# Matmuls over 64 rows grouped by twos of upper and lower halves, and the last steps before the experts' second table reordered

## The chip, the cores and the metric

One core of one Trainium2 chip runs the kernel. The metric is the device time of the whole program in microseconds (us), lower is better. The core has a matrix engine (PE, with its weight loads, PEld, shown apart), a vector engine (DVE), a scalar engine (ACT), GpSimd (POOL), and SyncE (SP), which issues DMAs. SBUF is the working memory of 128 partitions; PSUM, in eight banks, takes what PE writes.

## The reference

A decoder layer over 256 tokens of width 1024, all in float32:

```
h = rmsnorm(x);  proj = h @ w_in        # retention q,k,v,gate | attention q,k,v | two merge gates
A = groupnorm(retention(rq, rk, rv)) * silu(rg) @ ret_w_branch    # 8 heads, keys of 64, values of 128
B = softmax(mq mk^T + bias, causal) mv @ moba_w_branch            # 8 heads of 64
x = x + (sigmoid(ga) * A + sigmoid(gb) * B) @ w_out
h2 = rmsnorm(x)                         # then experts: 8 heads pick 16 of 16384 each
x = x + sum over picked e of gate_e * gelu(h2 . u[e]) * v[e]
```

Retention works in two chunks of 128 tokens: scores inside a chunk times a decay, and for the second chunk a product with the state that the first one left (`kv`).

## The kernel before

The program is one long list of instructions, in the order in which the Python code makes them; each engine takes its own in that order.

**Mixer** (to about 262 us). The projections are split into pieces of 256 rows of weights. For each piece `i` the loop loads, cuts the float32 weights into two parts (`cut`: ACT line 146, DVE line 147), does 12 matmuls (`products`, L229 to L231 or L238 to L240) and then calls `pump()`. `pump` takes one step of each of up to three tasks: Python generators that stop at each `yield`. Such a step is called a visit here. `attention()` and `retention()` are tasks. Their small matmuls go into PSUM tiles `side`, a ring of four banks; DVE or ACT then takes the bank's content away.

Heads of width 64 lie by twos in 128 partitions: head half `c = 0` in partitions 0 to 63, `c = 1` in 64 to 127 (`b = slice(c * 64, (c + 1) * 64)`). So attention's scores (L360), retention's scores (L423) and the product with the state (L440) are matmuls over 64 rows. All others near them are over 128 rows. A float32 matmul of the program stands as two instructions in the trace. Before the change a visit deals with one half at a time; in retention, L438 (128 rows) and L440 (64 rows) take turns into the same piece of a bank.

**Experts**. For 128 chunks `c` of the table u (loop at L1209): chunk's load, transposes (L711), products (L1224). Beside it the rows that some tokens picked are fetched one by one (`fetch`, a POOL DMA, L990) and used on DVE: `gather_step()` makes one fetch and one use, `gather(n)` adds `n` to a credit and makes a step for each whole one. For rows of v the use is a sum (L1075, into `accx` and then `vacc`), which comes six fetches later. In the last chunks the first pieces of the second phase are prepared: `cut_v` splits a chunk of v (ACT L146, DVE L147), `cut_w` a pair of columns of the gate matrix W (ACT L1197, DVE L1198). The place where the loop over u ends and the one over v (L1261) begins is called the seam. In the loop over v each chunk has 16 matmuls (L1257, L1258), or plain ones (L1255) for ten pairs of chunks, and a `gather(GATHER_V)`.

Of the kernel before, what the change touches and what calls it, by code (L numbers as in the profile page):

```python
# [19 lines left out]
OP = mybir.AluOpType  # L20
AX = mybir.AxisListType

P = 128
S = 256
# [3 lines left out]
H = 8  # L28
NK = 128
# [7 lines left out]
NW = NG + NXP * NXV  # L37
ND = S - NW
RING = 6
GATHER_V = 0.6  # L40
GATHER = 1.04
GATHER_G = 1.36
RAWS = 6
# [31 lines left out]
def layer_kernel(ctx, tc, x, mix_norm_g, w_in, ret_w_branch, moba_q_gain, moba_k_gain, moba_w_branch,  # L75
# [3 lines left out]
    V, A, G, T = nc.vector, nc.scalar, nc.gpsimd, nc.tensor  # L79
# [16 lines left out]
    def side():  # L96
        return psum.tile([P, 512], F32, name="side", bufs=4)
# [83 lines left out]
    def t4(shape, name, dt=F32):  # L181
        return wk.tile(shape, dt, name=name, tag="t4", bufs=3)
# [75 lines left out]
    bias = ap.tile([P, H, S], F32, name="bias", tag="b8d")  # L258
# [90 lines left out]
    def attention():  # L349
        ssum = wk.tile([P, NT, H], F32, name="ssum")  # L350
        for t in range(NT):
            w = (t + 1) * P
            pr = wk.tile([P, H, S], F32, name="pr")
            nh = 512 // w
            for i0 in range(0, H, nh):
                p = side()
                for j in range(nh):
                    c, hp = divmod(i0 + j, 4)
                    b = slice(c * 64, (c + 1) * 64)
                    T.matmul(p[:, j * w:(j + 1) * w], mqk[0][b, hp, t * P:(t + 1) * P], mqk[1][b, hp, :w],  # L360
                             start=True, stop=True)
                V.tensor_tensor(pr[:, i0:i0 + nh, :w], p.rearrange("p (j k) -> p j k", j=nh),
                                bias[:, i0:i0 + nh, S - w:], op=OP.add)
                yield
            sm = wk.tile([P, H], F32, name="smx")
            V.tensor_reduce(sm, pr[:, :, :w], axis=AX.X, op=OP.max, negate=True)
            for h in range(H):
                A.activation(pr[:, h, :w], pr[:, h, :w], AF.Exp, bias=sm[:, h:h + 1], accum_out=ssum[:, t, h:h + 1])
                if h % 4 == 3:
                    yield  # L370
            rs = wk.tile([P, H], F32, name="rs")
            V.reciprocal(rs, ssum[:, t, :])
            yield
            po = side()
            for kt in range(t + 1):
                prT = t4([P, H, P], "prT")
                for q in range(2):
                    p = side()
                    for j in range(4):
                        T.transpose(p[:, j * P:(j + 1) * P], pr[:, 4 * q + j, kt * P:(kt + 1) * P], ident)  # L380
                    A.activation(prT[:, 4 * q:4 * q + 4, :], p.rearrange("p (j i) -> p j i", j=4), AF.Copy)
                yield
                for i in range(H):
                    h = 2 * (i % 4) + i // 4
                    T.matmul(po[:, h * 64:(h + 1) * 64], prT[:, i, :], mv[:, kt, h * 64:(h + 1) * 64],
                             start=(kt == 0 and i == 0), stop=(kt == t), skip_group_check=True)
            at = t2([P, 512], "at")
            for c in range(2):
                V.tensor_tensor(at.rearrange("p (i c d) -> p c i d", c=2, d=64)[:, c],
                                po.rearrange("p (i c d) -> p c i d", c=2, d=64)[:, c],  # L390
                                rs[:, 4 * c:4 * c + 4, None].to_broadcast([P, 4, 64]), op=OP.mult)
            yield
            p = side()
            for c in range(4):
                T.transpose(p[:, c * P:(c + 1) * P], at[:, c * P:(c + 1) * P], ident)
            split_to(ah[0][:, :, t * P:(t + 1) * P], al[0][:, :, t * P:(t + 1) * P],
                     p.rearrange("p (c q) -> p c q", c=4))
            yield
# [7 lines left out]
    def retention():  # L406
        for q in range(2):
            p = side()
            for j in range(2):
                hp = 2 * q + j  # L410
                T.matmul(p[:, j * S:(j + 1) * S], kdec[:, hp * P:(hp + 1) * P], rv[0][:, hp * S:(hp + 1) * S],
                         start=True, stop=True)
            A.activation(kv[:, 2 * q:2 * q + 2, :], p.rearrange("p (j e) -> p j e", j=2), AF.Copy)
            yield
        for t in range(NT):
            s = slice(t * P, (t + 1) * P)

            st = t4([P, H, P], "st")
            for c in range(2):
                b = slice(c * 64, (c + 1) * 64)  # L420
                p = side()
                for j in range(4):
                    T.matmul(p[:, j * P:(j + 1) * P], rqk[1][b, j, s], rqk[0][b, j, s], start=True, stop=True)  # L423
                V.tensor_tensor(st[:, 4 * c:4 * c + 4, :], p.rearrange("p (j i) -> p j i", j=4),
                                decay[:, 4 * c:4 * c + 4, :], op=OP.mult)
                yield
            st6 = wk.tile([P, H, 6], F32, name="st6")
            mvv = wk.tile([P, H, 2], F32, name="mvv")
            va = wk.tile([P, H], F32, name="va")
            nm = wk.tile([P, H], F32, name="nm")  # L430
            os_ = []
            for c in range(2):
                b = slice(c * 64, (c + 1) * 64)
                p = side()
                for j in range(4):
                    h = 2 * j + c
                    d = p[:, j * P:(j + 1) * P]
                    T.matmul(d, st[:, 4 * c + j, :], rv[t][:, h * P:(h + 1) * P], start=True, stop=(t == 0))  # L438
                    if t:
                        T.matmul(d, rqdT[b, j, :], kv[b, j, c * P:(c + 1) * P], start=False, stop=True)  # L440
                for j in range(4):
                    V.bn_stats(st6[:, 4 * c + j, :], p[:, j * P:(j + 1) * P])
                os_.append(p)
                yield
            for i in range(H):
                V.bn_aggr(mvv[:, i, :], st6[:, i, :])
            V.tensor_scalar(va, mvv[:, :, 1], EPS, None, op0=OP.add)  # L447
            r = rsqrt_(wk, va, [P, H], "gn")
            yield
            V.scalar_tensor_tensor(nm, mvv[:, :, 0], -1.0, r, op0=OP.mult, op1=OP.mult)  # L450
            for c in range(2):
                for j in range(4):
                    h, i = 2 * j + c, 4 * c + j
                    A.activation(ret[:, t, h * P:(h + 1) * P], os_[c][:, j * P:(j + 1) * P], AF.Identity,
                                 bias=nm[:, i:i + 1], scale=r[:, i:i + 1])
                yield
# [301 lines left out]
    for t in range(NT):  # L758
        for q in range(2):
# [4 lines left out]
            p = side()  # L764
# [422 lines left out]
    def cut_v(c):  # L1187
        if c < NK:
            hi, lo = hi_tile(), lo_tile()
            split_to(hi, lo, v_raw.pop(c))  # L1190
            v_cut[c] = (hi, lo)

    def cut_w(c):

        if c < NK:
            w = cw[:, c // 2 % 2]
            A.activation(w[:, :, :ND], W[:, c:c + 2, :], AF.Copy)  # L1197
            V.tensor_tensor(w[:, :, ND:], W[:, c:c + 2, :], w[:, :, :ND].bitcast(F32), op=OP.subtract)  # L1198
            w_cut[c] = w
# [9 lines left out]
    for c in range(NK):  # L1209
        load_to(len(pieces) + c + TAHEAD)  # L1210
        rows_x(c)
        gates_finish()
        transpose_u(c + TAHEAD)
        if c and c % 2 == 0:
            product_evac(c - 2, pa)
        if c == SCRATCH:
            while any(g in chain for g in topk_all):
                chain_step(1.0)
        if c % 2 == 0:
            pa = acc(0)  # L1220
        uT = u_T.pop(c)
        for k in range(KC):
            n = c % 2 * NA
            T.matmul(pa[:, n:n + NA], uT[:, k * P:(k + 1) * P], hTf[:, k], start=(c % 2 == 0 and k == 0),  # L1224
                     stop=(k == KC - 1), skip_group_check=True)
        pump()
        if c < NK - 3:
            gather(gs["pace"])
        chain_step(BUDGET)

        if c == NK - 4:
            while chain:
                chain_step(9.0)
                gates_finish()
            cw = cp.tile([P, 2, D], F32R, name="cw", tag="b8")[:, :, :4 * ND].rearrange("p s (c t) -> p s c t", c=2)
        if c >= NK - 3:
            load_to(len(pieces) + c + 3)
        if c == NK - 3:
            cut_v(0)
        elif c == NK - 2:  # L1240
            cut_w(0)
        elif c == NK - 1:
            cut_v(1)
    product_evac(NK - 2, pa)

# [136 lines left out]
```

## Time and profile before

| | us |
|---|---|
| median of 3 runs | 975.61 (974.99 to 977.25) |
| the profiled execution | 976.44 |
| its span in the trace | 974.7 |
| PE busy in the span | 965.4 |

The rows below come from the one profiled execution. Its time is its span and 1.74 us around it. [...]

### The profile page before, as it was taken

Reading aid. Unit: us, or ns where it says so; the run is one execution under the profiler, and the core shown is the slowest. Engines: PE = TensorE matmul, PEld = TensorE weight load, DVE = VectorE, ACT = ScalarE, POOL = GpSimd, SP = SyncE. Lnnn points to the kernel's source line nnn. Section 1 sums busy time; section 2 is a strip of 40 time slices with the busy share of each in tenths; the row PEclk is TensorE's granted clock in tenths of the full one; section 3 lists DMA queues with packets and bytes.
Section 4 is the critical chain, followed back from the end, with each engine's and each line's share of the span. In section 5 each row is a group of like instructions: output and inputs, shape, how many; then the busy total and the mean of one; then the engine's idle time right before and its main releaser. Section 6 shows DMA issues by size and latency. Waiting matters only on the chain.

```text
span 974.7 us, 19119 instructions
## 1 busy us (share of the span) xinstructions
PE 965.4 (99%) x7208; PEld 922.7 (95%) x7208; DVE 782.4 (80%) x1487; ACT 516.3 (53%) x943; POOL 359.2 (37%) x303
## 2 busy tenths in 40 slices
PE   8999999999999999999999999999999999999998
PEld 6887887988999999999999999999999999999997
DVE  6667666988678997999789898845888888888886
ACT  5544554544554445444567676975454445544443
POOL 2421000000202446534446676746444434435410
PEclk9999999999999999999999999999999999999999
DMA  8876777995698999999998989989999999999993
GB/s 298 244 195 203 220 218 215 298 317 192 215 370 330 406 390 337 377 380 392 353 397 328 373 330 383 397 299 393 368 394 396 357 384 377 377 389 379 370 323 99
DMA packets 108043, 318.30 MB, mean 327 GB/s; under 512 B 11277, under 2 KB 21398, under 8 KB 107823
## 3 DMA queue, kind: packets, MB, share of 16 engines
q1 hardware_dynamic: 64524, 184.43, 52.9%
q0 software_dynamic: 32528, 115.54, 31.6%
q10 hardware_dynamic: 10898, 17.11, 5.7%
q8 instruction: 57, 0.93, 0.4%
q14 instruction: 36, 0.29, 0.1%
HBM read 306.47 MB, written 12.09 MB: 327 GB/s over the span
## 4 chain that ended last, share of the span: by engine, by line
PE 92%; DMA 4%; issue 2%; POOL 1%; DVE 1%; ACT 0%; SPq 0%; ACTq 0%; DVEq 0%; POOLq 0%
PE acc L1224 19%; PE side L711 9%; PE acc L1257 8%; PE side L1257 8%; PE acc L229 6%; PE acc L231 5%; PE acc L230 5%; PE acc L1153 4%; PE acc L1258 4%; PE side L1258 4%; PE acc L239 3%; PE acc L238 3%; PE acc L240 3%; PE side L1255 2%; PE acc L1255 2%
## 5 line engine op out<-in xcount | busy, mean ns | idle before, releaser
L990 POOL DMA_INDIRECT rows<-in_peer_u_dram,eg x86 | 105.9, 1232 | 78.2 <-DVE rows L1001 34.3
L990 POOL DMA_INDIRECT rows<-in_peer_v_dram,eg x54 | 79.6, 1475 | 107.1 <-DVE vacc L1075 91.7
L711 PE MATMUL side<-ident,raw_ring 128*128 128x128 f32 x816 | 107.1, 274 | 0.9 <-DMA raw_ring<-in_peer_u_dram 0.9
L711 PEld LDWEIGHTS side<-ident,raw_ring 128*128 128x128 f32 x816 | 98.7, 190 | 1.0 <-issue 1.0
L1001 DVE SCALAR_TENSOR_TENSOR rows<-rows,h 128x1024 f32<-128x1024 f32 x43 | 52.6, 1230 | 8.1 <-DMA rows<-in_peer_u_dram,eg 8.1
L1075 DVE SCALAR_TENSOR_TENSOR vacc<-rows,av,vacc 128x1024 f32<-128x1024 f32 x43 | 55.0, 1278 | 0.1
L1168 ACT ACTIVATE W<-acc 128x512 f32<-128x512 f32 (+17 forms) x44 | 28.0, 637 | 31.8 <-DVE W L1166 31.0
L1183 POOL TENSOR_TENSOR W<-W,gl 128x256 f32<-128x256 f32 (+16 forms) x29 | 27.1, 935 | 46.2 <-ACT gl L1182 40.5
L1197 ACT ACTIVATE cw<-W 128x352 fp32r<-128x352 f32 x54 | 26.5, 492 | 28.5 <-PE acc L1258 25.6
L1113 DVE TENSOR_TENSOR oh_buf<-niota,tT 128x512 f32<-128x512 f32 x44 | 33.1, 753 | 6.6 <-ACT tT L1135 6.6
L1198 DVE TENSOR_TENSOR cw<-W,cw 128x352 fp32r<-128x352 f32 x54 | 28.1, 519 | 9.6 <-ACT cw L1197 9.4
L571 POOL DMA_DIRECT2D x1d<-xt x1 | 0.7, 657 | 89.2 <-DVE xt L553 89.2
L153 POOL TENSOR_TENSOR gny<-va,minus_half 128x8 f32<-128x8 f32 x2 | 3.3, 1654 | 75.3 <-DVE va L447 75.3
L1119 ACT ACTIVATE oh_buf<-oh_more,tT 128x128 f32<-128x128 bf16 x88 | 29.3, 425 | 0.0
L1119 ACT ACTIVATE oh_more<-oh_more,tT 128x128 f32<-128x128 bf16 x88 | 29.3, 425 | 0.0
L1166 DVE TENSOR_TENSOR W<-acc,W 128x280 f32<-128x280 f32 (+16 forms) x32 | 24.7, 773 | 5.2 <-PE acc L1153 3.9
L1255 PE MATMUL side<-W,raw_ring 128*128 128x176 f32 x160 | 27.4, 314 | 0.0
L1224 PE MATMUL acc<-hTf,raw_ring 128*128 128x128 f32 x224 | 27.3, 275 | 0.0
L1255 PE MATMUL acc<-W,raw_ring 128*128 128x176 f32 x160 | 27.1, 313 | 0.0
L1224 PEld LDWEIGHTS acc<-hTf,raw_ring 128*128 128x128 f32 x224 | 26.1, 192 | 0.0
L1075 DVE SCALAR_TENSOR_TENSOR accx<-rows,av,accx 128x1024 f32<-128x1024 f32 x9 | 11.5, 1281 | 16.5 <-DMA rows<-in_peer_v_dram,eg 16.5
L1255 PEld LDWEIGHTS acc<-W,raw_ring 128*128 128x128 f32 x160 | 24.7, 190 | 0.0
(2619 smaller groups left out, 3487.4 us busy)
## 6 DMA issues: line engine op xcount, KB each, us to landing
raw_ring<-in_peer_v_dram SPq DMA_DIRECT2D x128, 512.0 KB, 8.5
raw_ring<-in_peer_u_dram SPq DMA_DIRECT2D x102, 512.0 KB, 8.8
raw_ring<-in_w_in_dram SPq DMA_DIRECT2D x52, 512.0 KB, 4.5
raw_ring<-in_peer_w_q_dram SPq DMA_DIRECT2D x16, 512.0 KB, 7.7
raw_ring<-turned SPq DMA_DIRECT2D x14, 512.0 KB, 9.0
W<-in_peer_u_dram SPq DMA_DIRECT2D x12, 512.0 KB, 10.3
raw_ring<-in_ret_w_branch_dram SPq DMA_DIRECT2D x8, 512.0 KB, 8.3
raw_ring<-in_w_out_dram SPq DMA_DIRECT2D x8, 512.0 KB, 6.5
```

Of the source, the lines that this page charges most:

```text
L229: T.matmul(o[t], xh[:, s], wh, start=(k == 0), stop=False)
L230: T.matmul(o[t], xh[:, s], wl, start=False, stop=False)
L231: T.matmul(o[t], xl[:, s], wh, start=False, stop=(k == kc - 1))
L711: T.transpose(p[:, k * P:(k + 1) * P], r.rearrange("p (i k) -> p k i", k=KC)[:, 4 * q + k], ident)
L990: G.indirect_dma_start(out=r, out_offset=None, in_=tab, in_offset=bass.IndirectOffsetOnAxis(ap=eg[:, j:j + 1], axis=0))
L1001: V.scalar_tensor_tensor(r, r, 1.0, h, op0=OP.mult, op1=OP.mult, accum_out=av[:, j:j + 1])
L1075: V.scalar_tensor_tensor(a, r, av[:, j:j + 1], a, op0=OP.mult, op1=OP.add)
L1119: A.activation(o1[:, j], o1b[:, :, j], AF.Copy, scale=tT[:, t, 1, k + j:k + j + 1])
L1224: T.matmul(pa[:, n:n + NA], uT[:, k * P:(k + 1) * P], hTf[:, k], start=(c % 2 == 0 and k == 0), stop=(k == KC - 1), skip_group_check=True)
L1255: T.matmul(o[b][:, :ND], vh[:, n], w, start=False, stop=False, skip_group_check=True)
L1257: T.matmul(o[b][:, :2 * ND], vh[:, n], w, start=(c == 0), stop=False, skip_group_check=True)
L1258: T.matmul(o[b][:, :ND], vl[:, n], w[:, :ND], start=False, stop=(c == NK - 1), skip_group_check=True)
```

## The change

Three edits in `attention()` and `retention()`: two banks are taken at once, and the matmuls of the lower and the upper half take turns, one of each. Where the values of the second chunk are made, all eight products over 128 rows (L438) come first, then the eight over 64 rows (L443), accumulating; before, they took turns, four and four in each of two visits. DVE's work on the second bank stays one visit later. At the seam, `gather` stops three chunks sooner, `cut_w(0)` goes into chunk NK - 3 ahead of `cut_v(0)`, `cut_v(1)` moves from NK - 1 to NK - 2, and loads run one chunk further ahead from NK - 5 on. `GATHER_V` goes from 0.6 to 0.62.

```diff
-GATHER_V = 0.6
+GATHER_V = 0.62
...
-            for i0 in range(0, H, nh):
-                p = side()
+            for i0 in range(0, 4, nh):
+                ps = [side() for _ in range(2)]
                 for j in range(nh):
-                    c, hp = divmod(i0 + j, 4)
-                    b = slice(c * 64, (c + 1) * 64)
-                    T.matmul(p[:, j * w:(j + 1) * w], mqk[0][b, hp, t * P:(t + 1) * P], mqk[1][b, hp, :w],
-                             start=True, stop=True)
-                V.tensor_tensor(pr[:, i0:i0 + nh, :w], p.rearrange("p (j k) -> p j k", j=nh),
-                                bias[:, i0:i0 + nh, S - w:], op=OP.add)
-                yield
+                    for c in range(2):
+                        b = slice(c * 64, (c + 1) * 64)
+                        T.matmul(ps[c][:, j * w:(j + 1) * w], mqk[0][b, i0 + j, t * P:(t + 1) * P],
+                                 mqk[1][b, i0 + j, :w], start=True, stop=True)
+                for c in range(2):
+                    n = slice(4 * c + i0, 4 * c + i0 + nh)
+                    V.tensor_tensor(pr[:, n, :w], ps[c].rearrange("p (j k) -> p j k", j=nh),
+                                    bias[:, n, S - w:], op=OP.add)
+                    yield
...
+            ps = [side() for _ in range(2)]
+            for j in range(4):
+                for c in range(2):
+                    b = slice(c * 64, (c + 1) * 64)
+                    T.matmul(ps[c][:, j * P:(j + 1) * P], rqk[1][b, j, s], rqk[0][b, j, s], start=True, stop=True)
...
-                    T.matmul(d, st[:, 4 * c + j, :], rv[t][:, h * P:(h + 1) * P], start=True, stop=(t == 0))
-                    if t:
-                        T.matmul(d, rqdT[b, j, :], kv[b, j, c * P:(c + 1) * P], start=False, stop=True)
+                    T.matmul(os_[c][:, j * P:(j + 1) * P], st[:, 4 * c + j, :], rv[t][:, h * P:(h + 1) * P],
+                             start=(j == 0), stop=(t == 0), skip_group_check=True)
+            for j in range(4 if t else 0):
+                for c in range(2):
+                    b = slice(c * 64, (c + 1) * 64)
+                    T.matmul(os_[c][:, j * P:(j + 1) * P], rqdT[b, j, :], kv[b, j, c * P:(c + 1) * P], start=False,
+                             stop=True, skip_group_check=True)
...
-        if c < NK - 3:
+        if c < NK - 6:
             gather(gs["pace"])
...
-        if c >= NK - 3:
+        if c >= NK - 5:
             load_to(len(pieces) + c + 3)
         if c == NK - 3:
+            cut_w(0)
             cut_v(0)
         elif c == NK - 2:
-            cut_w(0)
-        elif c == NK - 1:
             cut_v(1)
```

On PE, at attention's first scores (`mqk` holds the heads' keys and queries; `side_513` and `side_514` are two banks), the changed kernel has one visit in which the banks, and with them the halves, take turns:

```order
L272 MATMUL side_505<-ident_89,qn_436 128x128 x4
L360 MATMUL side_513<-mqk1_119,mqk0_118 128x128
L360 MATMUL side_514<-mqk1_119,mqk0_118 128x128
L360 MATMUL side_513<-mqk1_119,mqk0_118 128x128
L360 MATMUL side_514<-mqk1_119,mqk0_118 128x128
L360 MATMUL side_513<-mqk1_119,mqk0_118 128x128
L360 MATMUL side_514<-mqk1_119,mqk0_118 128x128
L360 MATMUL side_513<-mqk1_119,mqk0_118 128x128
L360 MATMUL side_514<-mqk1_119,mqk0_118 128x128
L229 MATMUL acc_530<-rhi__447,hh_84 128x512
```

Before, four of one half stood here, and the four of the other half one visit (12 matmuls) later. For 256 keys the visits go from four to two, for retention's scores from four to two.

On PE, at the values of retention's second chunk (`st` are the scores, `kv` the state), the first of two visits before against the only one now:

```order
 L231 MATMUL acc<-rhi__1253,hl 128x512
-L438 MATMUL side<-rv_126,st 128x128
-L440 MATMUL side<-kv,rqdT 128x128
-L438 MATMUL side<-rv_126,st 128x128
-L440 MATMUL side<-kv,rqdT 128x128
-L438 MATMUL side<-rv_126,st 128x128
-L440 MATMUL side<-kv,rqdT 128x128
-L438 MATMUL side<-rv_126,st 128x128
-L440 MATMUL side<-kv,rqdT 128x128
+L438 MATMUL side<-rv_126,st 128x128 x8
+L443 MATMUL side<-kv,rqdT 128x128 x8
 L229 MATMUL acc<-rhi__1293,hh 128x512
```

The products over 64 rows no longer stand between those over 128 rows.

On DVE, at the seam (`accx` takes the sums of fetched rows of v, `rlo` is the lower part of a chunk of v, `cw` the pair of W), before:

```order
L1075 SCALAR_TENSOR_TENSOR accx<-rows__7048,av,accx 128x1024
L1075 SCALAR_TENSOR_TENSOR accx<-rows,av,accx 128x1024 x4
L1075 SCALAR_TENSOR_TENSOR accx<-rows__7157,av,accx 128x1024
L147 TENSOR_TENSOR rlo__7274<-raw_ring,rhi__7273 128x1024
L1198 TENSOR_TENSOR cw<-W,cw 128x2x176
L147 TENSOR_TENSOR rlo__7302<-raw_ring,rhi__7301 128x1024
```

and now:

```order
L1079 SCALAR_TENSOR_TENSOR accx<-rows__7048,av,accx 128x1024
L1079 SCALAR_TENSOR_TENSOR accx<-rows,av,accx 128x1024
L1202 TENSOR_TENSOR cw<-W,cw 128x2x176
L147 TENSOR_TENSOR rlo__7264<-raw_ring,rhi__7263 128x1024
L147 TENSOR_TENSOR rlo__7281<-raw_ring,rhi__7280 128x1024
```

Eight sums stood ahead of the seam's first splits, four do now; the other four come in the loop over v. The split of W moved ahead of both chunks of v.

## Rows read from the trace of the kernel before

**Rows 1.** The page's first part: busy time, share, instructions of each engine.

```profile
PE 965.4 (99%) x7208; PEld 922.7 (95%) x7208; DVE 782.4 (80%) x1487; ACT 516.3 (53%) x943; POOL 359.2 (37%) x303
```

**Rows 2.** PE's waits over the whole span: total, times, longest, in us.

```profile
PE side L1257 <- DVE cw L1198: 1.0, 1, 1.0
```

**Rows 3.** Timeline of PE at a visit of retention's scores: start, length (us), operands, count.

```profile
117.28 0.39 PE L231 MATMUL acc<-rhi__923,hl 128*128 128x512 f32 x1
117.50 0.60 PE L395 MATMUL side<-ident,at 128*128 128x128 f32 x4
118.03 1.16 PE L423 MATMUL side<-rqk,rqk 64*128 64x128 f32 x8
119.12 0.50 PE L229 MATMUL acc<-rhi__959,hh 128*128 128x512 f32 x1
119.45 0.40 PE L230 MATMUL acc<-rlo__960,hh 128*128 128x512 f32 x1
```

**Rows 4.** Timeline of PE at the values of retention's second chunk.

```profile
150.42 0.48 PE L440 MATMUL side<-kv,rqdT 64*128 64x128 f32 x2
150.84 0.49 PE L438 MATMUL side<-rv,st 128*128 128x128 f32 x2
151.25 0.49 PE L440 MATMUL side<-kv,rqdT 64*128 64x128 f32 x2
...
153.34 0.50 PE L229 MATMUL acc<-rhi__1293,hh 128*128 128x512 f32 x1
```

**Rows 5.** Lines 360, 423, 440 by themselves: count, shortest, median, longest ns, forms.

```profile
L360 PE MATMUL side<-mqk,mqk x32: 272/374/480, 48.2 to 90.3; 64*128 64x128 f32 x16, 64*128 64x256 f32 x16
L423 PE MATMUL side<-rqk,rqk x32: 272/272/373, 118.0 to 147.1; 64*128 64x128 f32 x32
L440 PE MATMUL side<-kv,rqdT x16: 272/322/373, 150.4 to 159.2; 64*128 64x128 f32 x16
```

**Rows 6.** The chain that ended last, in order of time: start, share of it (us).

```profile
48.27 1.08 PE side L360 x8
...
68.11 1.73 PE side L385 x16
76.72 1.06 PE side L360 x4
```

**Rows 7.** Timeline of PE at the seam; in brackets idle time before, and its releaser.

```profile
677.74 1.95 PE L1224 MATMUL acc<-hTf,rhi__7218 128*128 128x128 f32 x16
679.53 1.95 PE L1224 MATMUL acc<-hTf,rhi__7251 128*128 128x128 f32 x16
682.46 0.40 PE L1257 MATMUL side<-cw,rhi__7273 128*128 128x352 f32 x1 [0.98 <-DVE cw L1198]
682.69 0.24 PE L1258 MATMUL side<-cw,rlo__7274 128*128 128x176 f32 x1
682.77 0.35 PE L1257 MATMUL side<-cw,rhi__7273 128*128 128x352 f32 x1
```

**Rows 8.** Timeline of DVE ahead of the seam.

```profile
667.90 1.28 DVE L1075 SCALAR_TENSOR_TENSOR accx<-rows,av,accx 128x1024 f32<-128x1024 f32 x1 [1.24 <-DMA rows<-in_peer_v_dram,eg]
...
678.94 1.80 DVE L1075 SCALAR_TENSOR_TENSOR accx<-rows__7157,av,accx 128x1024 f32<-128x1024 f32 x1 [1.27 <-DMA rows__7157<-in_peer_v_dram,eg]
680.66 1.21 DVE L147 TENSOR_TENSOR rlo__7274<-raw_ring,rhi__7273 128x1024 fp32r<-128x1024 f32 x1
681.80 0.51 DVE L1198 TENSOR_TENSOR cw<-W,cw 128x352 fp32r<-128x352 f32 x1
```

**Rows 9.** Windows of the loop over v: busy us by engine, PE's clock, DMA share, GB/s.

```profile
682.00:940.00 258.00, 257.54 (x1862) 257.57 (x1863) 218.05 (x214) 121.80 (x146) 112.61 (x71) 1.00 0.99 377
727.00:753.00 26.00, 26.00 (x190) 26.00 (x189) 23.11 (x23) 12.28 (x15) 10.47 (x8) 1.00 1.02 398
```

**Rows 10.** Timeline of DVE, two places in the mixer.

```profile
53.92 0.69 DVE L362 TENSOR_TENSOR pr<-side,bias 128x512 f32<-128x512 f32 x1 [5.90 <-DMA bias<-skew]
...
147.74 0.68 DVE L424 TENSOR_TENSOR st<-side,decay 128x512 f32<-128x512 f32 x1
```

More of the change, by code (lines that the diff above doesn't have):

```diff
@@ L418, in retention @@
             st = t4([P, H, P], "st")
-            for c in range(2):
[L420 to L424, printed above, removed]
+            ps = [side() for _ in range(2)]
[3 more added lines that the diff above has]
+                    T.matmul(ps[c][:, j * P:(j + 1) * P], rqk[1][b, j, s], rqk[0][b, j, s], start=True, stop=True)
+            for c in range(2):
+                V.tensor_tensor(st[:, 4 * c:4 * c + 4, :], ps[c].rearrange("p (j i) -> p j i", j=4),
                                 decay[:, 4 * c:4 * c + 4, :], op=OP.mult)
@@ L430, in retention @@
             nm = wk.tile([P, H], F32, name="nm")
-            os_ = []
+            os_ = [side() for _ in range(2)]
             for c in range(2):
-                b = slice(c * 64, (c + 1) * 64)
-                p = side()
                 for j in range(4):
                     h = 2 * j + c
-                    d = p[:, j * P:(j + 1) * P]
-                    T.matmul(d, st[:, 4 * c + j, :], rv[t][:, h * P:(h + 1) * P], start=True, stop=(t == 0))
-                    if t:
-                        T.matmul(d, rqdT[b, j, :], kv[b, j, c * P:(c + 1) * P], start=False, stop=True)
+                    T.matmul(os_[c][:, j * P:(j + 1) * P], st[:, 4 * c + j, :], rv[t][:, h * P:(h + 1) * P],
[5 more added lines that the diff above has]
+                             stop=True, skip_group_check=True)
+            for c in range(2):
                 for j in range(4):
-                    V.bn_stats(st6[:, 4 * c + j, :], p[:, j * P:(j + 1) * P])
-                os_.append(p)
+                    V.bn_stats(st6[:, 4 * c + j, :], os_[c][:, j * P:(j + 1) * P])
                 yield
```

## Prediction

> **What bounds the kernel now.** I read the busy times first: PE is busy for 965.4 of 974.7 us and its weight loads nearly as long [rows 1], so whatever shortens PE's own stream shortens the program, as long as nothing new makes PE wait. Then PE's waits: at the seam it stands for 1.0 us on DVE's split of W [rows 2]. Then PE's timeline where the diff is. There a "busy" PE hides lost time: between two neighbours the starts lie further apart than either needs. That is where I look for the change's main part.
>
> **Part 1: fewer changes between 128 and 64 rows.** Undisturbed, instructions of 128 columns start 0.111 us apart (16 of L1224 in 1.79 us [rows 7]), those of 512 columns some 0.23 us (117.28 to 117.50 [rows 3]). From L231 to L230 in [rows 3] that makes 0.23 + 4 x 0.111 + 8 x 0.111 + 0.23 = 1.79 us; the starts lie 119.45 - 117.28 = 2.17 us apart. The 0.38 us too much belong to one change to 64 rows and one back. In [rows 4] a change comes after every second instruction: 150.42 to 151.25 is 0.83 us for four instructions, which alone need 0.44, so 0.39 us for two changes; over the whole visit, 150.42 to 153.34, it is 2.92 us for 14 further instructions (1.55 us) and seven changes, 0.195 each. Both places say 0.19 to 0.195 us a change. It isn't a price of the bank, since L438 and L440 write the same one, and in [rows 7] L1258 and the next L1257 write different banks 0.08 us apart.
>
> Counting: before, attention has 2 visits of 128 keys and 4 of 256, retention's scores 4; each visit is entered and left, 20 changes. The values of the second chunk have 8 in each of two visits, 16. Together 36. The changed kernel has 1 + 2 + 2 such visits and one of values, 6 visits, 12 changes. 24 are gone: 24 x 0.193 = **4.6 us**, all on PE's stream, which sets the end.
>
> **Part 2: two halves side by side.** 40 matmuls, 80 instructions, are over 64 rows: 64 of 128 columns and 16 of 256 [rows 5]. Of them, neighbours of the same half start 0.111 and 0.217 us apart (8 in 1.08 and 4 in 1.06 us, less one change of 0.19 [rows 6]), no quicker than over 128 rows. Nowhere in the trace do two halves follow each other without a change of size in between, so what taking turns brings has to be bounded. From below: nothing, if halves simply queue. From above: both halves at once, half of 64 x 0.111 + 16 x 0.217 = 10.6, so 5.3 us. Two rows lie between. L385, of 64 columns, takes 1.73 us for 16, 0.108 each [rows 6], as long as 128 columns do: something other than the columns paces it, presumably the weights. If that goes on one by one for both halves, only the 256-column ones gain, 16 x (0.217 - 0.108) = 1.7, less some 0.3 where a visit's last one has no partner: 1.4 us. The closest two starts that rows show are 0.08 us [rows 7]; if that is what PE can issue, the 128-column ones gain 64 x (0.111 - 0.08) = 2.0 and the wide ones the same 1.7, less 0.5 for the six visits' ends: 3.2 us. I take **3.2 us**, as the row that shows a pace of issue, and keep 0 and 5.3 for the range.
>
> [...]
>
> What queues behind this: the second bank's DVE work now comes one visit after its matmuls, so a bank is held some 3 us longer. The ring has four banks, and the visits take two of them. The first adds wait for the bias till 53.92 in any case [rows 10], with PE three pieces further on work that is already cut. The values of the second chunk now need both halves' scores at once; DVE had the second ones at 147.74 + 0.68 = 148.4, and PE came to the values at about 150.1, two instructions ahead of [rows 4]. PE will be there about 1 us sooner, and still late enough. Cost nothing; if a bank is missed, up to 0.7 us (one such DVE instruction) at each of a few places.
>
> **Part 3: the seam.** PE ends the u loop's matmuls about 681.5 and idles 0.98 us, until DVE's split of W ends at 681.80 + 0.51 [rows 7, 8]. DVE was late because a sum waited for its fetched row till 678.94 and took 1.80, and the splits queued behind it. Now the fourth sum (667.90) is the last ahead of the splits, DVE is free from 669.2, and W's split goes first. W's split and two chunks' lower parts are 0.51 + 2 x 1.21 = 2.9 us, and from 677.74, where the last but one chunk's matmuls begin, there are 3.7 us to the seam; the first matmul needs only two of the three. So **1.0 us** is gained. Next late at the seam would be the second chunk of v, needed some 2.5 us after the first (8 pairs of matmuls of up to 0.31 us, 682.46 to 682.77 [rows 7]): no wait.
>
> **Part 4: four sums and four fetches moved into the loop over v** (the price of part 3, and what the 0.62 does). DVE gets 4 x 1.28 = 5.1 us more in a stage where it is busy for 218 of 258 us [rows 9]: 86.5 instead of 84.5%. The fetches are 4 x 0.52 MB, 5.6 us of transfer at 377 GB/s, in a stage with a DMA share of 0.99. Spread over 258 us they ask for 8 GB/s more, 385, and the stage reaches 398 in one window [rows 9]. I cost it at nothing, hidden behind PE's matmuls; if that cover is gone it is up to 5.6 us. Loading v a chunk sooner asks for no more bytes, and the sums still end ahead of the step that needs them (L1295, four chunks from the end).
>
> **Sum.** 4.6 + 3.2 + 1.0 = 8.8 us. The profiled execution took 976.4 us, so 967.6; the runs' median lies 0.8 lower, so I forecast **966.8 us** for the median. All the rest of the program is tied to PE's place in its stream (loads, fetches and choices are made per piece or chunk), so a mixer that ends sooner shifts it whole.
>
> **Rivals.**
> - *The halves gain little or nothing from each other.* For it: same-half neighbours show no gain from 64 rows, and L385's pace. Then 4.6 + 1.0, with 0 to 1.4: 968.6 to 970.0.
> [...]
> - *The loop over v is held by DMA.* For it: share 0.99. It would give back up to 5.6 of the 8.8: 972.4. Against it: 398 GB/s in a window, and PE is busy for 257.54 of the 258 us from 682, the rest being the seam's own wait [rows 9].
> - *The change of half costs what the change of size costs.* This one ends on the other side. Taking turns makes 7 changes of half in attention's first visit, 3 + 3 in the next two, 7 + 7 in retention's scores and 7 in the values, 34. At 0.193 that is 6.6 us against 5.6 gained by parts 1 and 3: 1.0 us slower, 976.6. It decides from 0.165 us per change on; at 0.22 the program would be slower by over 0.2%. Against it: in [rows 4] what changes is the number of rows, both ways at the same price, while no row has a change of half.
> - *The 0.19 us isn't saved,* as it belongs to something that stays: then only 1.0 us and perhaps some overlap, about 974.6.
>
> **How the numbers follow.** Overlap in part, my forecast: 0.35; full overlap 0.2; little or none 0.28; DMA or missed banks give half back 0.07; halves cost as changes 0.07; nothing saved 0.03. The range reaches from full overlap, less the runs' own 0.6 us below their median (964.1), to no overlap with 1 us of new waits (971.0); that leaves out the last three, under 2 in 10. Faster by over 0.2% (1.95 us, about what a measurement can tell from no change): 0.90. Within it: 0.06, from the cases of changes of half and of nothing saved. Slower: 0.04, changes of half that cost more than 0.22 us.
>
> **What would show it.** Ten visits over 64 rows become six. Part 1: the starts from L231 to L230 around a visit still hold 0.38 us beyond their instructions, but the values of the second chunk take 3 to 4 us in all instead of twice 3.3. Part 2: sixteen instructions over 64 rows in a visit span clearly under 16 x 0.111 = 1.8 us; 1.8 says they queue, about 0.9 says full overlap, above 2.5 that halves cost. Part 3: L1257 at the seam without idle time ahead. Part 4: no wait of PE between the seam and the end. I'd be wrong if PE's waits showed DVE or ACT in the mixer (banks), or DMA in the loop over v.

## The result, and the profile after

The median of six runs is 968.08 us (965.88 to 970.73) after and 976.43 us (974.16 to 979.53, six runs) before, a ratio of 0.9914 with a 95% interval of 0.9898 to 0.9930: 8.35 us faster, where 966.8 us was forecast. The profiled execution took 968.42 us, with a span of 966.7; the granted clock was 0.999 of full speed in it, as in the one before. The page's busy times of the kernel after:

```profile
PE 956.2 (99%) x7208; PEld 916.6 (95%) x7208; DVE 781.5 (81%) x1487; ACT 517.6 (54%) x943; POOL 366.2 (38%) x303
```

PE is busy for 9.2 us less than in [rows 1]. That is more than the span lost, so PE now waits more somewhere. PE's waits of the kernel after (total, times, longest; two at the program's start, about as long as before, and those of 0.4 us or less are left out):

```profile
PE side L387 <- ACT prT L383: 0.9, 1, 0.9
PE side L397 <- DVE at L391: 0.9, 1, 0.9
PE side L715 <- DMA raw_ring<-in_peer_u_dram: 0.6, 1, 0.6
PE side L1260 <- DVE cw L1202: 0.5, 1, 0.5
```

The first two are in the mixer, on ACT and DVE: what the forecast had named as a sign that it would be wrong. The first profile of the kernel before has neither; two further traces with the old mixer have a smaller wait at the first place (L385, which is L387 here), shown under e6. The last is no longer at the seam but in the loop over v, at 714.06. Lines below some 360 moved by two to four; L425 was L423 before, L443 was L440.

The visit of retention's scores, to be held against [rows 3] (timeline of PE, kernel after):

```profile
116.07 0.39 PE L231 MATMUL acc<-rhi__923,hl 128*128 128x512 f32 x1
116.30 0.60 PE L397 MATMUL side<-ident,at 128*128 128x128 f32 x4
116.83 1.16 PE L425 MATMUL side<-rqk,rqk 64*128 64x128 f32 x16
117.92 0.50 PE L229 MATMUL acc<-rhi__959,hh 128*128 128x512 f32 x1
118.25 0.39 PE L230 MATMUL acc<-rlo__960,hh 128*128 128x512 f32 x1
```

Sixteen instructions of two halves now take the place that eight of one half took: 1.16 us in both, and from L231 to L230 it is 2.18 us against 2.17. Line 425 by itself, kernel after, in a stretch of 0.01 us from 116.84 on (count, shortest, median, longest ns, first and last start):

```profile
L425 PE MATMUL side<-rqk,rqk x2: 373/373/373, 116.8 to 116.8; 64*128 64x128 f32 x2
```

Both have the 373 ns of a visit's first instruction, and both have started by then. Records of neighbours overlap anyway (272 ns long and 0.111 us apart), so it is the starts that count: by the single records each lower and upper one start 0.007 us apart, their weight loads too, and the next such pair follows 0.111 us later (0.216 with 256 columns; 0.213 and 0.314 behind a visit's first pair). The values of the second chunk, to be held against [rows 4]:

```profile
146.31 1.95 PE L438 MATMUL side<-rv,st 128*128 128x128 f32 x16
148.18 1.16 PE L443 MATMUL side<-kv,rqdT 64*128 64x128 f32 x16
149.27 0.50 PE L229 MATMUL acc<-rhi__1293,hh 128*128 128x512 f32 x1
```

From 146.31 to 149.27 is 2.96 us in all, in place of two visits of about 3.2.

To see where the time went, each trace is cut at four instructions of PE: its first attention score (L360), its first matmul after the mixer (L585 before, L589 after), its first of the loop over v (L1257 before, L1260 after; L1259 in e2, L1256 in e4, L1261 in e3 and e9), and its last. The table gives the three stretches in us, for all the kernels below. e1 to e4 ran on one chip, e5 to e8 on a second, e9 to e11 on a third.

| kernel | mixer | loop over u | loop over v | span |
|---|---|---|---|---|
| before | 213.83 | 420.42 | 288.37 | 974.7 |
| before, second profile (e10) | 214.20 | 418.22 | 288.37 | 972.5 |
| after | 206.47 | 418.80 | 289.38 | 966.7 |
| after, second profile (e11) | 205.33 | 418.61 | 288.38 | 963.9 |
| e1, halves in turn | 207.31 | 418.82 | 289.51 | 967.5 |
| e2, sizes mixed | 207.48 | 418.02 | 288.39 | 965.6 |
| e3, mixer's edits alone | 206.62 | 418.78 | 288.38 | 965.8 |
| e4, seam's edits alone | 214.67 | 418.33 | 288.77 | 973.6 |
| e5, bias sooner | 204.93 | 419.68 | 288.61 | 965.1 |
| e6, turns by GpSimd | 205.02 | 417.97 | 288.37 | 963.0 |
| e7, pace 0.60 | 206.39 | 418.28 | 288.38 | 965.3 |
| e8, e5 and e6 together | 203.75 | 419.17 | 288.38 | 963.8 |
| e9, e8 with the old seam | 203.75 | 419.93 | 288.37 | 964.4 |

Between the first profiles of before and after the mixer gives 7.36 us, the loop over u 1.62, and the loop over v takes back 1.01. The second profile of before has the same code and a loop over u that is 2.20 us shorter: differences of that size in this column say nothing by themselves. Two places make up that difference: the seam's wait of [rows 2], with which this column ends (1.05 us from start to start), and a chunk of u that landed late at 492.65 (1.04 us), which the second profile has neither of:

```profile
PE side L711 <- DMA raw_ring<-in_peer_u_dram: 0.9, 1, 0.9
```

The mixer of the same code agrees within 0.84 us before (e4 has it too) and 1.29 us after (e3 and e7 have it too).

### The profile page after: what moved, and what is told of

Read it like the earlier page. It is cut to its first block, busy times and chain, and to the rows that moved or that the text cites. A ratio compares the mean times of both kernels' runs of the same rounds, so it can differ in the third digit from the quotient of the medians.

```text
span 966.7 us, 19122 instructions
## 1 busy us (share of the span) xinstructions
PE 956.2 (99%) x7208; PEld 916.6 (95%) x7208; DVE 781.5 (81%) x1487; ACT 517.6 (54%) x943; POOL 366.2 (38%) x303
## 4 chain that ended last, share of the span: by engine, by line
PE 90%; DMA 4%; DVE 2%; issue 1%; ACT 1%; POOL 1%; ACTq 0%; SPq 0%; DVEq 0%; POOLq 0%
PE acc L1228 23%; PE side L715 10%; PE acc L1260 8%; PE side L1260 8%; PE acc L229 4%; PE acc L231 4%; PE acc L230 4%; PE acc L1157 4%; PE acc L1261 3%; PE side L1261 3%; PE acc L239 3%; PE acc L238 3%; PE acc L240 3%; PE side L1258 2%; PE acc L1258 2%; DMA raw_ring<-in_peer_u_dram 1%
## 5 line engine op out<-in xcount | busy, mean ns | idle before, releaser
L994 POOL DMA_INDIRECT rows<-in_peer_v_dram,eg x54 | 86.5, 1602 | 91.6 <-DVE vacc L1079 66.6
L1228 PE MATMUL acc<-hTf,raw_ring 128*128 128x128 f32 x224 | 27.3, 275 | 0.0
L1228 PEld LDWEIGHTS acc<-hTf,raw_ring 128*128 128x128 f32 x224 | 26.1, 192 | 0.0
L1258 PEld LDWEIGHTS side<-W,raw_ring 128*128 128x128 f32 x160 | 24.3, 190 | 0.0
```

Of the source, the lines that this page charges most:

```text
L994: G.indirect_dma_start(out=r, out_offset=None, in_=tab, in_offset=bass.IndirectOffsetOnAxis(ap=eg[:, j:j + 1], axis=0))
L1258: T.matmul(o[b][:, :ND], vh[:, n], w, start=False, stop=False, skip_group_check=True)
```

## The experiments

The ratios below are to the kernel before on the same chip, with 95% intervals.

**e1: the halves one after the other.** In each 64-row visit all of the lower half's matmuls come first, then the upper half's; nothing else changes.

```diff
-                for j in range(nh):
-                    for c in range(2):
+                for c in range(2):
+                    for j in range(nh):
```

> The changed kernel, but in each visit over 64 rows the four matmuls of the lower half come first and then the four of the upper half, still in two banks and in one visit. Theory (the halves run at once only where they take turns): 16 instructions of 128 columns in a visit span about 1.8 us and not 0.9, but for one overlapped pair at the border of the halves; the six visits together get 4.5 to 5 us longer than in the changed kernel. Since the changed kernel lost some 2.6 us of its gain in the mixer to waits that a later PE doesn't meet, the program gets 2 to 5 us slower than it: 970 to 973 us. Rival (the matrix engine looks ahead and lets the halves run at once in any order, or the gain is one of fewer changes of size alone): visits as short as in the changed kernel, same time, about 968.

Measured: 969.56 us (968.21 to 970.73), ratio 0.9927 (0.9909 to 0.9945). Timeline of PE, e1:

```profile
115.34 0.60 PE L397 MATMUL side<-ident,at 128*128 128x128 f32 x4
115.87 1.71 PE L425 MATMUL side<-rqk,rqk 64*128 64x128 f32 x16
117.51 0.50 PE L229 MATMUL acc<-rhi__959,hh 128*128 128x512 f32 x1
```

From L425 to L229 it is 1.64 us against 1.09 with the halves taking turns. Had they queued, it would be 0.89 more than 1.09, eight starts of 0.111. In the single records the lower half goes alone for 0.55 us; then the upper half's first instruction starts at 116.423, beside the lower half's fifth at 116.418, and the last four of the lower run beside the upper's. So neither the theory (1.8 us) nor the rival (1.09) holds whole: the overlap belongs to the halves, and taking turns earns 0.55 us of the 0.89 in a visit of 128 columns, about 2.2 us over the four such visits. The visits of 256 columns, of four and four, gained their whole overlap without taking turns (1.14 us for eight here, 1.13 after). In both forms the upper half's first starts beside the lower half's fourth from the end. The mixer is 0.84 us longer than after and not 2.2, because the wait of 0.9 us at L397 is gone. That has two parts: PE comes there 0.55 us later, and in this execution DVE's first add, which e5 shows to set this wait, came 0.8 us sooner (6.20 us behind the first score, 7.00 after). By time alone e1 and the change aren't told apart; the visit tells it.

**e2: sizes mixed again.** At the values of the second chunk two 128-row products and two 64-row ones take turns: 8 changes of size where the change has 2.

```diff
             for j in range(4):
                 for c in range(2):
...
-            for j in range(4 if t else 0):
-                for c in range(2):
+                for c in range(2 if t else 0):
```

> The changed kernel, but in the values of the second chunk two products over 128 rows and two over 64 rows take turns (halves still by turns, still one visit): 8 changes of size there and not 2. Theory (0.193 us for each change of size, both ways): this visit takes 6 x 0.193 = 1.2 us more than the 2.97 us from the first product over 128 rows to the next piece, so about 4.1, and each pair of products over 64 rows still starts together. Rival (the price of before came from halves that followed each other without a partner, not from the change of size): the visit stays within 0.3 us of 2.97. The program: 0 to 1.2 us slower than the changed kernel, too little to tell by its time alone.

Measured: 967.9 us (966.69 to 972.34), ratio 0.9919 (0.9897 to 0.9942). Timeline of PE, e2 (L442 is the 64-row product):

```profile
145.87 0.60 PE L438 MATMUL side<-rv,st 128*128 128x128 f32 x4
146.40 0.49 PE L442 MATMUL side<-kv,rqdT 64*128 64x128 f32 x4
146.82 0.71 PE L438 MATMUL side<-rv,st 128*128 128x128 f32 x4
...
149.59 0.49 PE L442 MATMUL side<-kv,rqdT 64*128 64x128 f32 x4
150.01 0.50 PE L229 MATMUL acc<-rhi__1293,hh 128*128 128x512 f32 x1
```

The same 32 instructions take 4.14 us in place of 2.96: 1.18 us for six more changes, 0.197 each. The mixer is longer than after by 1.01 us; the time doesn't show it, since the loops over u and v were 0.78 and 0.99 us shorter in this trace. The price of a change of size stands.

**e3 and e4: each part alone.** e3 has the mixer's three edits with the seam and the pace of before; e4 has the seam and the pace with the mixer of before. The lines in which e3 differs from the change:

```diff
-GATHER_V = 0.62
+GATHER_V = 0.6
...
-        if c < NK - 6:
+        if c < NK - 3:
...
-            cut_w(0)
             cut_v(0)
```

> The edits to attention and retention alone; seam and the pace of 0.6 as before. Theory (mixer 7.4 us sooner, of a PE stream shortened by 9.8, and the rest as before): the mixer's last matmuls come 7.4 us sooner, the seam shows its 1.0 us wait on the split of W again, the loop over v has no new wait: about 969 us against 976.4. Rival (the 1.0 us that the changed kernel lost in the first chunks of v comes from a mixer that ends sooner, or is DMA that varies from run to run): new waits of some 1 us in the loop over v here too, 970.

> The edits at the seam and the pace of 0.62 alone; attention and retention as before. Theory (four sums moved away from the seam free 1.2 us there, and come back as waits on late loads of v, 1.0 us in the changed kernel): mixer as before, no wait at the seam, waits of up to 1 us in the first dozen chunks of v: 975.2 to 976.4, no change that can be told from none. Rival (the wait in the loop over v belongs to one run of DMA and not to the moved sums): 975.2, with no wait after the seam.

Measured: e3 967.55 us (966.22 to 968.32), ratio 0.9903 (0.9884 to 0.9923), as much as the whole change; e4 975.79 us (974.2 to 977.8, twelve runs), ratio 0.9998 (0.9986 to 1.0009), no change. e3's PE idles for 0.03 us at the seam, though its seam is that of before; e4's loop over v is 0.39 us longer than with the old seam, at 720 and 796 us and not in the first dozen chunks, so neither the theory nor the rival of e4 holds whole. So the seam's 1.0 us, which I had counted, isn't in the time.

**e5: the bias sooner.** The bias rows' loads are issued two visits earlier, from POOL's queue (at 30.0 us and not 40.5).

```diff
-        for _ in range(5):
+        for _ in range(3):
             yield
```

> The change as it is, with the bias rows' loads issued earlier on POOL's queue (3 yields ahead of them in place of 5). Theory: in the trace after the change the first 8 us won by 73 us melt to nothing because ScalarE and VectorE start the first scores' softmax only when the bias has landed (first add at 55.15 us, 53.92 before). Then the first add starts near 49 to 51 us, TensorE's waits on the exps at 64 us and of 0.9 us at the transposes near 71 to 73 us go or shrink below 0.3, TensorE stands 1.0 to 1.6 us further ahead at 74 us than in the trace after the change, and the time is about 966.6 us (ratio to before 0.990). Rival: the chain of VectorE and ScalarE itself sets that stretch, not its start; then the waits stay, and so does the time, 968.1 us.

Measured: 966.14 us (965.12 to 967.37), ratio 0.9899 (0.9885 to 0.9913). First the chain as it is after the change: DVE's first add, DVE's scaling of the attention output (L391), and the transposes on PE that read it.

```profile
55.15 0.69 DVE L364 TENSOR_TENSOR pr<-side,bias 128x512 f32<-128x512 f32 x1 [7.21 <-PE acc L231]
...
72.15 0.74 DVE L391 TENSOR_TENSOR at<-side,rs 128x256 f32<-128x256 f32 x2
73.04 0.63 PE L397 MATMUL side<-ident,at 128*128 128x128 f32 x4 [0.89 <-DVE at L391]
```

The same two places in the kernel before:

```profile
70.92 0.74 DVE L389 TENSOR_TENSOR at<-side,rs 128x256 f32<-128x256 f32 x2
72.94 0.60 PE L395 MATMUL side<-ident,at 128*128 128x128 f32 x4
```

From the first add to the scaling it is 17.00 us in both kernels (70.92 - 53.92 and 72.15 - 55.15); before, the scaling was done 1.3 us ahead of PE. After the change PE's scores of both banks were made by 49.3 us. The add started at 55.15 all the same, no sooner than the 53.92 of [rows 10]. This row names PE as the releaser; in the second profile of the same kernel (e11) it is the bias:

```profile
53.68 0.69 DVE L364 TENSOR_TENSOR pr<-side,bias 128x512 f32<-128x512 f32 x1 [6.10 <-DMA bias<-skew]
```

With the bias sooner (e5):

```profile
49.21 0.69 DVE L364 TENSOR_TENSOR pr<-side,bias 128x512 f32<-128x512 f32 x1 [1.41 <-PE side L360]
...
68.44 0.75 DVE L391 TENSOR_TENSOR at<-side,rs 128x256 f32<-128x256 f32 x2 [0.43 <-issue]
...
71.44 0.60 PE L397 MATMUL side<-ident,at 128*128 128x128 f32 x4
```

The add follows the scores, the scaling ends 2.2 us ahead of the transposes, and their wait is gone. The mixer is 1.54 us shorter than in the first profile after, 0.40 shorter than in the second (e11), and 1.46 shorter than e7's, the change's mixer on the same chip. The rival falls: it was the chain's start, not its length. The time alone doesn't show it: its interval overlaps those of the change and of e7, and the same goes for e6 and e8.

**e6: the turns' early loads from GpSimd's queue.**

```diff
-                nc.scalar.dma_start(early[0][(m + 1) % 2][32 * g:32 * g + 32].rearrange("a (b d) -> a b d", b=4), src[g])
+                nc.gpsimd.dma_start(early[0][(m + 1) % 2][32 * g:32 * g + 32].rearrange("a (b d) -> a b d", b=4), src[g])
```

> The change as it is, with the four early loads of the turns issued from GpSimd's queue and no longer from ScalarE's. Theory: the TensorE wait of 0.9 us near 104.5 us on ScalarE's copies of the transposed probabilities is there because ScalarE spends 3.25 us on issuing these loads from 100.58 us on, which the earlier work of TensorE now catches. Then that wait goes, all that follows starts about 0.9 us sooner, and the time is 967.1 us. Rival: the copies are late by their own length; then the wait stays near 0.9 us and the time at 968.1 us. What could spoil it: GpSimd's queue has the loads behind its own work, and they land later.

Measured: 966.1 us (964.76 to 971.69), ratio 0.9915 (0.9896 to 0.9933). The place after the change, ACT and PE (ACTq is the issuing of DMAs by ACT):

```profile
100.55 1.07 ACT L146 ACTIVATE rhi__923<-raw_ring 128x1024 fp32r<-128x1024 f32 x1
100.58 3.25 ACTq L726 DMA_DIRECT2D h<-in_peer_u_dram  x4
103.88 1.08 ACT L383 ACTIVATE prT<-side 128x512 f32<-128x512 f32 x2 [2.26 <-PE acc L231]
...
104.53 2.00 PE L387 MATMUL side<-mv,prT 128*128 128x64 f32 x16 [0.94 <-ACT prT L383]
```

The copies that PE waits for begin 0.05 us after ACT's last issue. In e6 ACT issues none of them:

```profile
99.88 1.06 ACT L146 ACTIVATE rhi__923<-raw_ring 128x1024 fp32r<-128x1024 f32 x1
100.85 1.07 ACT L383 ACTIVATE prT<-side 128x512 f32<-128x512 f32 x2
...
102.73 1.89 PE L387 MATMUL side<-mv,prT 128*128 128x64 f32 x16
```

The copies come 3 us sooner and PE doesn't wait. The mixer is 1.45 us shorter than in the first profile after, 1.38 shorter than e7's. The wait at L397 stays at 0.9 us here, and in e5 that at L387 does: two causes.

This wait isn't wholly new. With the mixer of before, e10 has it with 0.25 us, and e4, whose issuing took longer:

```profile
101.61 4.04 ACTq L722 DMA_DIRECT2D h<-in_peer_u_dram  x4
105.70 1.08 ACT L381 ACTIVATE prT<-side 128x512 f32<-128x512 f32 x2 [3.05 <-DMA h<-in_peer_u_dram]
106.35 1.89 PE L385 MATMUL side<-mv,prT 128*128 128x64 f32 x15 [0.72 <-ACT prT L381]
```

The wait goes by the length of the issuing: 0, 0.25 and 0.72 us at 3.17, 3.60 and 4.04 us in the first profile before, e10 and e4; 0.89, 0.94 and 1.23 at 3.19, 3.25 and 3.54 in e11, the first profile after and e7. So there was no slack here to begin with, and at equal issuing the change adds about 1.0 us. It adds that in e5 too (0.95), though PE comes there 1.5 us sooner after its first score. What took this 1.0 us from ACT's place against PE no run separates; in the trace after, ACT stood 0.81 us for DVE's row maxima (L368) ahead of its exponentials, and before it didn't.

**e7: the old pace.** `GATHER_V` at 0.60 in the change, the rest as it is.

```diff
-GATHER_V = 0.62
+GATHER_V = 0.6
```

> The change as it is, with the pace of the fetches in the loop over v back at 0.60 (0.62 in the change). Theory: the 1.0 us that the loop over v loses near 709 to 714 us in the trace after the change is a transfer that lands late in some executions and not a matter of the pace: the kernel with 0.62 and another length of mixer shows no loss there. Then the time is that of the change, 968.1 us, within 0.2%, whatever this trace shows at that place. Rival: the later fetches bring the loss; then the waits near 710 to 714 us are gone, and the time is about 967.1 us.

Measured: 967.52 us (966.48 to 974.61), ratio 0.9931 (0.9907 to 0.9954): not to be told from the change. Its loop over v is 288.38, the 1.0 us is gone from the trace. But e11, e6, e8 and e2 have 0.62 and 288.37 to 288.39 as well. Of the eight traces with 0.62 the stretch is 288.37 to 289.51, 288.72 in the mean; of the five with 0.60 it is 288.37 or 288.38 in each. Four of these five have the old seam too, and only e7 has the new seam with 0.60, in one trace. So the seam's edits and the pace together look to cost 0.35 us on average, and up to 1.1; which of the two does isn't shown, and no time shows the cost.

**e8: both loads moved,** on top of the change.

> The earlier bias loads and the early loads of the turns from GpSimd's queue together, on top of the change. If both causes hold, the gains add: TensorE ends the mixer 2.0 to 2.5 us sooner than in the trace after the change, and the time is about 965.8 us (ratio to before 0.989). If the waits of the mixer come from the length of the softmax chain instead, it is that of the change, 968.1 us.

Measured: 967.27 us (963.93 to 967.86), ratio 0.9906 (0.9890 to 0.9921). The mixer is 2.72 us shorter than in the first profile after, 1.58 than in e11 and 2.65 than e7's, where 2.0 to 2.5 were expected; neither L387 nor L397 is among the waits. The time missed the expectation by 1.5 us, and by time e8 isn't ahead of e5 or e6: that the gains add is shown by the mixer alone.

**e9, e10, e11.** e9 is e8 with the seam and the pace of before. e10 and e11 are the kernels before and after once more.

> The change's matmuls by twos, the bias and turn loads issued sooner and from GpSimd's queue, and the seam and the pace of 0.60 of the kernel before. Theory: all that the change brings lies in the mixer, and the edits at the seam bring nothing that the time shows; then TensorE ends the mixer some 9 us ahead of the kernel before, and the time is about 966 us (ratio 0.989 to 0.990), not above that of the change. Rival: the seam's edits are worth the 1.0 us that I had for them; then about 967 us, with TensorE idle for about 1 us ahead of the first matmul of the loop over v.

> The kernel before, a second profile. If the wait of 1.0 us at the seam belongs to the order of the code, it is there again, 0.8 to 1.1 us; if it was a fetched row that landed late in that one execution, it is under 0.3 us or gone.

> The changed kernel, a second profile. The waits of 0.9 us at the transposes of the mixer, near 71 to 73 us and near 104.5 us, come back if they belong to the order of the work; the loss of 1.0 us in the loop over v near 710 to 714 us doesn't, if it was a late transfer of one execution.

Measured: e9 965.21 us (964.74 to 966.21), ratio 0.9883 (0.9867 to 0.9900), the lowest median of all; its mixer equals that of e8, and PE idles for 0.07 us at the seam, so the rival falls. e10 took 974.25 us and e11 965.72, one run each on the same chip, so how far e9 is ahead of the change isn't settled by time. The seam in e10, PE and DVE:

```profile
678.35 1.95 PE L1224 MATMUL acc<-hTf,rhi__7251 128*128 128x128 f32 x16
680.23 0.40 PE L1257 MATMUL side<-cw,rhi__7273 128*128 128x352 f32 x1
...
676.69 1.28 DVE L1075 SCALAR_TENSOR_TENSOR accx<-rows__7157,av,accx 128x1024 f32<-128x1024 f32 x1 [1.29 <-DMA rows__7157<-in_peer_v_dram,eg]
677.89 1.75 DVE L147 TENSOR_TENSOR rlo__7274<-raw_ring,rhi__7273 128x1024 fp32r<-128x1024 f32 x1
679.57 0.51 DVE L1198 TENSOR_TENSOR cw<-W,cw 128x352 fp32r<-128x352 f32 x1
```

The last sum starts 3.54 us ahead of PE's first matmul of the loop over v here, and 3.52 in [rows 7, 8]; but here PE was still at work. The split of W ends at 680.08 and PE's sixteen starts at 680.13 (678.35 + 16 x 0.111): the old order meets the seam with nothing to spare, and 1.0 us in the first profile was a row that landed that much later. After the change the same place reads, PE and DVE:

```profile
671.72 1.95 PE L1228 MATMUL acc<-hTf,rhi__7239 128*128 128x128 f32 x16
673.42 0.41 PE L1260 MATMUL side<-cw,rhi__7263 128*128 128x352 f32 x1
...
669.46 0.53 DVE L1202 TENSOR_TENSOR cw<-W,cw 128x352 fp32r<-128x352 f32 x1 [8.50 <-ACT cw L1201]
670.41 1.22 DVE L147 TENSOR_TENSOR rlo__7264<-raw_ring,rhi__7263 128x1024 fp32r<-128x1024 f32 x1 [0.42 <-ACT rhi__7263 L146]
```

The first two splits end at 671.63, 1.8 us ahead of PE. From the first of the last sixteen L1224 (L1228 after) to the first matmul of the loop over v it is 1.71 us in all nine traces with the new order, and 1.88, 1.98 and 2.02 in e10, e3 and e9 with the old one, 2.93 in the first profile before. So the new order is worth 0.2 to 0.3 us in three of these four, and 1.2 in one. The waits of e11:

```profile
PE side L387 <- ACT prT L383: 0.9, 1, 0.9
...
PE side L397 <- DVE at L391: 0.2, 1, 0.2
```

L387's is there again as it was, as the order of the work on ACT is the same; L397's is smaller, with a first add 1.07 us sooner (5.93 us behind the first score and not 7.00). The wait in the loop over v isn't there.

## Why the prediction was right, and which steps were off

**Part 1** held. Around a 64-row visit the starts still hold the 0.38 us of [rows 3], twelve changes are left, and e2 prices one at 0.197 us where I had 0.193; what makes a change cost that, no run shows. 24 x 0.193 = 4.6 us stands.

**Part 2** had the mechanism and the wrong size: I took 3.2 us, and it measured 5.3. 64 instructions of 128 columns now need 32 x 0.111 = 3.6 us, 16 of 256 need 8 x 0.216 = 1.7; together 5.3 in place of 10.6. The step that failed is the choice of the closest starts in [rows 7], 0.08 us, as what PE can issue. Those two instructions use the same 128 rows; they say nothing of two that use different rows, which start 0.007 us apart. That nothing starts closer than in those rows was an argument from a place where the thing couldn't have been seen. The rival that halves cost as changes do is excluded by the same starts: 0.007 us from one half to the other, against 0.197 us for a change of size. Full overlap, to which I had given 0.2, was right in this term; the 964.7 us that it makes (4.6 + 5.3 + 1.0 = 10.9 off 975.6) were missed because of the waits below.

Together parts 1 and 2 are worth 9.9 us. e8 and e9, in which nothing in the mixer makes PE wait anew, show it: 203.75 against the 213.83 us of the first profile before, 10.1 less. These three have the same idle time of PE in the mixer, 0.41 us at its end.

**"What queues behind this: cost nothing"** is the step that failed outright. The mixer of the change is 206.47, 205.33, 206.62 and 206.39 us (after, e11, e3, e7), 1.6 to 2.9 us more than e8's. I had written that the first adds wait for the bias till 53.92 in any case, and read it as cover. It is the opposite: this chain hangs on a DMA and not on PE and didn't follow when PE got faster (first add at 55.15 and 53.68 us after, 53.92 before), so PE ran into its end, 18 us later at L397 (0.9 and 0.2 us). The other wait, at L387, needs ACT's 3.2 us of issuing loads (e6); before, these ended just as PE came, or up to 0.7 us too late, and now PE comes some 1.0 us sooner against them. Banks, which I had named as the danger, are not what PE waits for in either. e5, e6 and e8 undo the two apart and together: 1.46, 1.38 and 2.65 us against e7 on the same chip. The claim in the sum that all else is tied to PE's place in its stream was wrong at these two places.

**Part 3** showed as forecast in the trace, with no idle time ahead of the first L1260, but the term of 1.0 us belongs to one execution: e4 shows nothing in time, and in e10, e3 and e9 the old order costs 0.2 to 0.3 us.

**Part 4** was costed at nothing; the traces show 0.35 us on average, not resolved by time. That is about as much as the seam gains in most executions.

So 4.6 + 5.3 + 0.2 - 0.35 is 9.75 us, less 1.6 to 2.9 for the two waits 6.9 to 8.2, against 8.35 by the medians; the rest is of the size of what the loop over u (1.0 us) and the old mixer's own wait at L385 (up to 0.8) move between executions. The forecast of 8.8 came out near by luck: 2.1 us of overlap not counted made up for 1.6 to 2.9 us of waits not counted and for a seam's gain of which most executions show about a quarter. What stays open is the loop over u: one late transfer moves it by 1.0 us between the two profiles before, and no experiment here tried to hold the transfers still.

## What to carry to other kernels

Before counting a gain on the bounding engine as whole, look for the work beside it that hangs on something else, a DMA's landing or an engine's issuing of DMAs (the waits of 0.9 us at L397 and at L387 here), and ask how many us ahead of the bounding engine it is where the two next meet (its slack); what the engine gains beyond that slack is lost there, however far on. A wait in one profile is a term of the sum only if the code's order makes it: a second profile of the same kernel costs one run and would have struck the seam's 1.0 us. The matmuls over half the rows were worth grouping twice here: once so that sizes change seldom (0.197 us a change), and once so that the two halves can run beside each other (starts 0.007 us apart, 5.3 us in all).

## What the runs showed of the hardware

Two 64-row instructions of different halves cost what one costs, weight loads included: pairs start 0.007 us apart, for 128 and for 256 columns, and from a visit's first start to what follows it is 1.09 us for sixteen against 1.08 for eight (128 columns), 1.06 for eight as for four (256).

In e1, PE did not take the two halves strictly in the program's order. Line 425 by itself in e1, from 115.88 to 116.40 and then from 116.42 to 116.75:

```profile
L425 PE MATMUL side<-rqk,rqk x4: 272/272/373, 115.9 to 116.3; 64*128 64x128 f32 x4
L425 PE MATMUL side<-rqk,rqk x8: 272/272/373, 116.2 to 116.7; 64*128 64x128 f32 x8
```

In the first stretch four start, 0.111 us apart or more. The second counts what runs in it, three of them started earlier; five start inside, where one half alone would make three in 0.33 us. Yet all eight of the lower half stand ahead of the upper half's first in the program. In the records the lower half's last instruction, the one that signals, starts at 116.753, and three of the upper half have started by then. The records' ends are modelled, so only the starts and the length of the visit, 1.64 us and not 1.98, are evidence.
